# Three causal attentions of a two-block transformer: pairs of heads in a pipeline, their half-array products alternating, in a pinned order of the matrix engine

## The chip, the core and the metric

The kernel runs on one core of a Trainium2 chip. A core has a matrix engine (TensorE, called PE in the profile), a vector engine (DVE), a scalar engine (ACT), GpSimd (POOL) and a sync engine (SP) that issues most DMAs. Each engine works through its own queue in order and waits at semaphores for the others. The metric is the time of one execution on the device in microseconds (us), lower is better; the median of the runs shown counts.

## What is computed

Two transformer blocks over 256 tokens of 1024 features, in float32. Block 1: attention (16 heads of 64 features, rotary positions; with one block of keys it is plain causal attention) beside a gated recurrence, cross attention to a memory, a feed-forward net. Block 2: two layers of feed-forward, mixer, feed-forward; the first mixer is NSA, the second differential attention. The three attentions that the change touches, shortened:

```
# block 1, per head h:        p = softmax(causal(q k^T / 8));  o = p v
# NSA, 16 query heads, 4 key heads; with 256 tokens all selected and window keys are in reach:
def nsa_mixer(h, ...):
    o_cmp, o_sel = nsa_compressed_selected(q, kc, vc, ks, vs, slopes)   # 15 compressed keys; 256 keys
    o_win = banded_attention(q, kw, vw, slopes, NSA_WINDOW)             # 256 keys
    g = sigmoid(gates)
    o = g[..., 0:1] * o_cmp + g[..., 1:2] * o_sel + g[..., 2:3] * o_win
    return o @ w_out
# differential attention, 8 heads, two score maps each, values of 128:
    p = masked_softmax(sc, dist >= 0)
    a = p[:, :, 0] - lmbda * p[:, :, 1]
    o = rmsnorm(a @ v, subln) * (1 - lam_init);  return o @ w_out
```

## The kernel before

Weights of some 280 MB stream through the core once. `proj` (line 320) loads a weight tile of 512 rows by 512 columns, and for each pair of 128-row chunks ACT makes a rounded copy (`wh`, line 354), DVE the remainder (`wl`, line 355), and PE twelve products of 128x128 by 512 columns: two chunks, two token tiles, three products each (lines 330, 334, 335). `proj` is a generator that yields after each weight tile (24 products).

The attentions work per head. `softmax_causal` (line 476) makes the causal scores in two blocks, 128 queries by 128 keys and 128 by 256, into one PSUM bank ("sc", two banks in turn), with 64 features as contraction: a half of the array's rows. DVE adds the bias and finds each row's extreme in one operation (line 485), ACT takes the exponential with its row sum (line 487). Then reciprocal and scaling on DVE, three 128x128 transposes on PE (line 508) with a copy to SBUF, and P@V, whose 64 output features use a half of the array's columns. Three stages do so:

- A, `attn_a` (line 634): 16 heads, woven with the remaining chunks of `qkv` and the first inputs of the recurrence (`weave`, rate 0.6 tiles a head).
- N, `attn_n` (line 1141), called for two halves m = 0, 1 of the heads: per key head and branch two heads (`par`), 16 pairs in all; `compressed_branch` (line 1099) is a small softmax over 16 blocks for 8 heads at once, its P@V (line 1170) joins the others in bank "on".
- D, `attn_d` (line 1243), two halves of four heads: two score maps a head, combined on DVE (lines 1252 to 1254), P@V with 128 features (lines 1257 to 1259).

The order of the engines' queues is made by the framework's scheduler, which moves instructions by its own cost model, except those wrapped in `late`, which keep the program's order among themselves. Before, only a few are pinned: deferred transposes (`tick`, line 254) and two products (`hold`). So weight products, scores, transposes and P@V of neighbouring heads are mixed as the scheduler sees fit. In A, N and D the weight products that do not depend on the attention are the filler.

Of the kernel before, what the change touches and what calls it, by code (L numbers as in the profile page):

```python
# [2 lines left out]

# [14 lines left out]
P = 128  # L18
# [10 lines left out]
def shape_constants():  # L29
# [28 lines left out]
    # heads as (group pair, kv head, parity of the group): head = 4 * kv head + 2 * group pair + parity  # L58
# [25 lines left out]
def tile_kernel(ctx: ExitStack, tc: tile.TileContext, A, out):  # L84
    nc = tc.nc
    V, SC, G, T = nc.vector, nc.scalar, nc.gpsimd, nc.tensor
    late = tc.keep_in_program_order

# [22 lines left out]
    class Feat:  # L111
        """[feature, token]: chunks of 128 features by 256 tokens, four chunks to a tile, made when first used."""
# [15 lines left out]
    class Tok:  # L128
        """[token, feature]: 2 x 128 tokens by 1024 features, 512 features to a tile, made when first used."""
# [16 lines left out]

    def wk(shape, s, bufs, dt=F32):
        tag, bufs = ("w2k", NW2K) if s in W2K else (s, bufs)
        return work.tile(shape, dt, name=nm(s), tag=tag, bufs=bufs)
# [8 lines left out]
    BS = {"sc", "sx", "cs", "ch", "dc"}  # L158
# [30 lines left out]
    def load_gains():  # L189
# [10 lines left out]
        # gains of 64, twice along the row  # L200
# [17 lines left out]
    def rsqrt(ms, n):  # L218
        """1/sqrt of ms [128, n] (any positive float32), by Newton steps."""
# [27 lines left out]
    # transposes wait for the vector engines: they are queued behind matrix products that do not  # L247
# [6 lines left out]
    def tick():  # L254
        for p in pending:
            p[0] -= 1
        if pending and pending[0][0] <= 0:
            pending.pop(0)[1](late)
# [61 lines left out]
    def proj(xT, w, nchunks, evac, lead=False, rows=None, pre=None, final=False):  # L320
        """evac(n, tt, psum) for each chunk of columns of x @ w."""
# [5 lines left out]
        def products(o, c, tt, h, l):  # L327
# [3 lines left out]
            if hold[0]:  # L331
                late(first)
                hold[0] -= 1
# [6 lines left out]
        for grp in groups:  # L340
# [4 lines left out]
            for k0, nk in units:  # L345
                for n in grp:
# [4 lines left out]
                    for c0, m in [(0, 1), (1, 1), (2, 2)] if early else [(c, min(2, nk - c)) for c in range(0, nk, 2)]:  # L351
# [5 lines left out]
                        if not by_tile:  # L357
# [4 lines left out]
                            tick()  # L362
                    if k0 + nk == kc:
# [5 lines left out]

    def run(*gens):  # L370
        for g in gens:
            for _ in g:
                pass

    def weave(main, fill, rate=None, at=()):
        """Emit `rate` units of fill for each step of main (or one after each of the steps `at`), then what is left."""
        acc = 0.0
        for i, _ in enumerate(main):
            acc += at.count(i + 1) if rate is None else rate
            while acc >= 1.0:  # L380
                next(fill, None)
                acc -= 1.0
        run(fill)

# [3 lines left out]
    def residual(xT, w, alpha, g, s, lead=True, rows=None):  # L388
        """x += alpha * (xT @ w): a generator; its result holds the next normed operand (split x^T * g) and 1/rms."""
# [55 lines left out]
    def to_T(src, blocks, dst, scale=None, age=2):  # L445
        """dst(b), dst(b + 1): transposes of the blocks of src(b, tt), times scale, for pairs of blocks."""
# [11 lines left out]
    def segment_norm(ps2, rs, nseg, extra=None):  # L458
        """For psum tiles of both token tiles: 1/rms over runs of 64 of (ps * rs), times rs (and extra)."""
# [16 lines left out]
    def softmax_causal(qT, kT, bias, mscale):  # L476
        """exp(mscale * (q k + bias) - its max) per row [128, 384] and the row sums [128, 2]."""
        ps = bank("sc")
        T.matmul(ps[:, 0:128], qT[:, 0:128], kT[:, 0:128], start=True, stop=True)  # L479
        T.matmul(ps[:, 128:384], qT[:, 128:256], kT[:, 0:256], start=True, stop=True)  # L480
# [3 lines left out]
        for tt, (a, b) in enumerate(((0, 128), (128, 384))):  # L484
# [4 lines left out]
        return p, sm  # L489

# [13 lines left out]
    def transpose_p(p, evac=evac_copy):  # L504
        """[t, (t0 s0 | t1 s0 | t1 s1)] to [s, same blocks]."""
# [3 lines left out]
        pT = wk([P, 384], "pT", 3)  # L509
# [19 lines left out]
    next(qkv)  # L529
    transposed_half(xa, 1, xT1h, xT1l, g1)  # L530
    next(qkv)
# [6 lines left out]
    # rotary tables, times 1/rms: [128, tt, 32]  # L538
# [65 lines left out]
    for _ in range(4):  # L604
        next(qkv)
# [10 lines left out]
    for _ in range(2):  # L616
        next(qkv)
    transpose_gains()

    # products of gains that meet in one contraction  # L620
# [11 lines left out]
    oTah, oTal = new_xT("oa")  # L632

    def attn_a():
        for pair in range(8):
            if pair == 4:
                flush()
            o = bank("o")
            for h2 in range(2):
                r = slice(h2 * 64, h2 * 64 + 64)  # L640
                h = 2 * pair + h2
                p, sm = softmax_causal(qTa(pair)[r], kTa(pair)[r], causal, 0.125)
                ri = tn([P, 2], "ri", 6)
                V.reciprocal(ri, sm)
                V.tensor_scalar(p[:, 0:128], p[:, 0:128], ri[:, 0:1], None, op0=ALU.mult)
                V.tensor_scalar(p[:, 128:384], p[:, 128:384], ri[:, 1:2], None, op0=ALU.mult)
                pT = transpose_p(p)
                T.matmul(o[r, 0:256], va(0, h * 64, 64), pT[:, 0:256], start=True, stop=False)  # L648
                T.matmul(o[r, 128:256], va(1, h * 64, 64), pT[:, 256:384], start=False, stop=True)
                yield  # L650
            split_evac(o[:, 0:256], oTah(pair), oTal(pair))

# [10 lines left out]
    def silu_tanh(ps, tt, dst):  # L663
        """2 * silu(ps * rstd)."""
# [15 lines left out]
    class Hgrn:  # L680
        """heads 4n..4n+3."""
# [57 lines left out]
        def head(self, hh_):  # L739
            """chunks of 128 tokens by binary levels, and the pair of chunks."""  # L740
# [72 lines left out]
    weave(attn_a(), fill_a(), 0.6)  # L813
# [33 lines left out]
    def fill1():  # L847
        yield from proj(xT1, w_in, cols(8192, 9216), evac_gate(gb))
        for _ in range(4):
            next(kv)  # L850
# [15 lines left out]
    next(kv)  # L866
    next(kv)

# [13 lines left out]
    next(qx)  # L882
    next(qx)
# [82 lines left out]
    def seg_T(ps2, nseg, dup, r2, dst, scale=None):  # L966
        """Normed runs of 64 (each twice if dup), then transposed to dst."""
# [58 lines left out]
    # compressed tokens  # L1026
# [7 lines left out]
    def compress(w1):  # L1034
        """keys on rows 0..63 of the hidden layer, values on rows 64..127: (head, 16 blocks)."""
# [55 lines left out]
        # for each kv head the keys of both parities, on the diagonal  # L1091
# [7 lines left out]
    def compressed_branch(m):  # L1099
        """P of the compressed branch for 8 heads, times gate / sum, transposed: [(kv head, 32), parity, 256 t]."""  # L1100
        psc = bank("cs")
        for tt in range(2):
            for hk in range(4):
# [3 lines left out]
        # the queries carry 1/slope: times the slope of each head again  # L1107
# [8 lines left out]
        # a row that sees no block has only -1e30: all its weights become 0  # L1116
# [10 lines left out]
                        mx.rearrange("p (a r) -> p a r", r=2)[:, :, :, None].to_broadcast([P, 8, 2, 16]), ALU.mult)  # L1127
        tp = bank("pct")
# [6 lines left out]
        return pcT  # L1135
# [5 lines left out]
    def attn_n(m):  # L1141
        pcT = None
        for hk in range(4):
            o = bank("on")
            for br in range(2):
                vv = vsw[br]
                pTs = []
                for par in range(2):
                    i = 4 * hk + 2 * m + par
# [177 lines left out]
```

## Time and profile before

| | |
|---|---|
| runs, us | 1727.02, 1727.28, 1731.16; median 1727.28 |
| profiled execution, span | 1724.7 us |
| PE busy | 1702.2 us, 99% |
| DVE busy | 1078.7 us, 63% |
| ACT busy | 898.4 us, 52% |
| stage A (first scores to last P@V) | 61.8 to 146.5 us |
| stage N | 929.4 to 1027.9 us |
| stage D, from the norm of its first keys | 1449 to 1525 us |

The span is the time from the first to the last instruction of the profiled execution; the timed runs hold some 2.6 us more around it. A PE instruction of float32 is shown as two passes, so a product appears twice in a row's count; a row of the timeline with x2 or x4 stands for several instructions, and its second number is the time from the start of the first to the modelled end of the last. Neighbouring products overlap by their modelled ends, so costs are read from start to start.

### The profile page before, as it was taken

The page shows a single profiled execution, that of the slowest core. Times are in us where ns is not written, and L with a number is a line of the kernel's source. Part 1 is how long each engine was busy: PE and PEld are TensorE (multiplying, and loading weights), DVE is VectorE, ACT ScalarE, POOL GpSimd, SP SyncE. Part 2 cuts the span into 40 slices and gives each one's busy share as a digit, 9 for nine tenths or more (in the row PEclk, how much of TensorE's full clock was granted, in tenths as well). Part 3 has the DMA queues.
Part 4 walks back from the last instruction along what each step waited for, and adds up shares of the span by engine and source line. Part 5 has one row for each costly group of instructions (what it writes and reads, how often), then busy time and mean ns, then how long its engine had stood idle before and what let it go on. Part 6 is the DMA issues. An engine that isn't in the chain of part 4 may idle for free.

```text
span 1724.7 us, 21866 instructions
## 1 busy us (share of the span) xinstructions
PE 1702.2 (99%) x8170; PEld 1366.3 (79%) x8170; DVE 1078.7 (63%) x2129; ACT 898.4 (52%) x1473; POOL 29.5 (2%) x49
## 2 busy tenths in 40 slices
PE   8999999999999999999999999999999999999999
PEld 6767888878878888888877667888888887778887
DVE  6866585766465555655577766555655557975554
ACT  5566456545454445544455655444444455765442
POOL 3100000000000000000000000000000000000000
PEclk9999999999999999999999999999999999999999
DMA  8333344245445555655574115555555554345554
GB/s 296 132 122 137 126 154 171 98 147 171 158 152 177 191 172 194 195 177 190 195 238 134 50 34 172 189 187 191 183 181 185 180 191 166 123 147 189 178 183 134
DMA packets 211226, 284.12 MB, mean 165 GB/s; under 512 B 8304, under 2 KB 136032, under 8 KB 211120
## 3 DMA queue, kind: packets, MB, share of 16 engines
q1 hardware_dynamic: 209024, 278.10, 48.8%
q0 software_dynamic: 1936, 4.57, 0.8%
q8 instruction: 64, 1.05, 0.2%
q14 instruction: 42, 0.34, 0.1%
q10 hardware_dynamic: 160, 0.07, 0.0%
HBM read 281.65 MB, written 1.05 MB: 164 GB/s over the span
## 4 chain that ended last, share of the span: by engine, by line
PE 93%; DVE 3%; ACT 2%; issue 1%; DMA 0%; POOL 0%; SPq 0%; ACTq 0%; DVEq 0%; POOLq 0%
PE mm L330 26%; PE mm L335 26%; PE mm L334 26%; PE am L774 1%; PE pT L508 1%; PE ht L436 1%; PE sc L480 1%; PE xt L272 1%; PE on L1163 1%; DVE wl L355 1%; PE sc L479 1%; PE tT L452 1%; ACT wh L354 1%; PE o L648 1%; PE dc L752 0%
## 5 line engine op out<-in xcount | busy, mean ns | idle before, releaser
L355 DVE TENSOR_TENSOR wl<-raw,wh 128x1024 fp32r<-128x1024 f32 (+1 forms) x523 | 636.8, 1219 | 478.4 <-ACT wh L354 477.7
L354 ACT ACTIVATE wh<-raw 128x1024 fp32r<-128x1024 f32 (+1 forms) x523 | 549.1, 1051 | 560.1 <-PE mm L335 544.2
L330 PE MATMUL mm<-wh,hh 128*128 128x512 f32 x440 | 172.6, 392 | 0.0
L335 PE MATMUL mm<-wh,hl 128*128 128x512 f32 x440 | 171.4, 389 | 0.0
L334 PE MATMUL mm<-wl,hh 128*128 128x512 f32 x440 | 171.3, 389 | 0.0
L330 PE MATMUL mm<-wh,x1h 128*128 128x512 f32 x288 | 115.7, 405 | 0.0
L334 PE MATMUL mm<-wl,x1h 128*128 128x512 f32 x288 | 114.6, 399 | 0.9 <-DVE wl L355 0.9
L335 PE MATMUL mm<-wh,x1l 128*128 128x512 f32 x288 | 113.4, 395 | 0.0
L335 PEld LDWEIGHTS mm<-wh,hl 128*128 128x128 f32 x440 | 82.6, 188 | 17.4
L330 PEld LDWEIGHTS mm<-wh,hh 128*128 128x128 f32 x440 | 82.6, 188 | 16.9
L334 PEld LDWEIGHTS mm<-wl,hh 128*128 128x128 f32 x440 | 82.7, 188 | 16.8
L427 ACT ACTIVATE silu<-mm,rstd 128x256 f32<-128x256 f32 x110 | 51.8, 475 | 62.3 <-PE mm L335 60.2
L330 PE MATMUL mm<-wh,xeh 128*128 128x512 f32 x176 | 70.0, 398 | 1.1 <-ACT xeh L280 1.1
L330 PE MATMUL mm<-wh,xbh 128*128 128x512 f32 x176 | 70.0, 398 | 1.1 <-ACT xbh L280 1.1
L330 PE MATMUL mm<-wh,xfh 128*128 128x512 f32 x176 | 69.7, 398 | 1.1 <-ACT xfh L280 1.1
L330 PE MATMUL mm<-wh,xch 128*128 128x512 f32 x176 | 69.8, 397 | 0.0
L330 PE MATMUL mm<-wh,xnh 128*128 128x512 f32 x176 | 69.6, 395 | 0.0
L335 PE MATMUL mm<-wh,xnl 128*128 128x512 f32 x176 | 68.7, 390 | 0.0
L334 PE MATMUL mm<-wl,xnh 128*128 128x512 f32 x176 | 68.7, 390 | 0.0
L334 PE MATMUL mm<-wl,xeh 128*128 128x512 f32 x176 | 68.7, 390 | 0.0
L335 PE MATMUL mm<-wh,xcl 128*128 128x512 f32 x176 | 68.6, 390 | 0.0
L334 PE MATMUL mm<-wl,xch 128*128 128x512 f32 x176 | 68.6, 390 | 0.0
(429 smaller groups left out, 3335.3 us busy)
## 6 DMA issues: line engine op xcount, KB each, us to landing
raw<-in_ffn_w_in_dram SPq DMA_DIRECT2D x176, 512.0 KB, 4.6
raw<-in_ffn_w_out_dram SPq DMA_DIRECT2D x40, 1024.0 KB, 4.8
raw<-in_w_in_dram SPq DMA_DIRECT2D x35, 1024.0 KB, 4.8
raw<-in_w_ffn_in_dram SPq DMA_DIRECT2D x44, 512.0 KB, 4.5
raw<-in_diff_w_in_dram SPq DMA_DIRECT2D x12, 1024.0 KB, 5.0
raw<-in_w_ffn_out_dram SPq DMA_DIRECT2D x10, 1024.0 KB, 4.8
raw<-in_wkv_x_dram SPq DMA_DIRECT2D x8, 1024.0 KB, 5.0
raw<-in_w_br_attn_dram SPq DMA_DIRECT2D x4, 1024.0 KB, 4.8
```

What stands on the lines that cost most here:

```text
L272: pin(T.transpose(tp[:, cc * 256 + tt * P:cc * 256 + (tt + 1) * P], src(tt, (c0 + cc) * P, P), ident))
L330: first = T.matmul(o, a, h, start=(c == 0), stop=False)
L334: T.matmul(o, a, l, start=False, stop=False)
L335: T.matmul(o, b, h, start=False, stop=(c == kc - 1))
L354: SC.activation(wh[:, :m, :wd], raw[:, c0:c0 + m, :wd], AF.Copy)
L355: V.tensor_tensor(wl[:, :m, :wd], raw[:, c0:c0 + m, :wd], f32(wh[:, :m, :wd]), ALU.subtract)
L427: SC.activation(s_, ps[:, 0:256], AF.Silu, scale=rs[:, tt:tt + 1])
L436: pin(T.transpose(tp[:, cc * 256 + t2 * P:cc * 256 + (t2 + 1) * P], hs[n, t2][:, cc * P:(cc + 1) * P], ident))
L452: pin(T.transpose(tp[:, i * 256 + tt * P:i * 256 + (tt + 1) * P], src(b + i, tt), ident))
L479: T.matmul(ps[:, 0:128], qT[:, 0:128], kT[:, 0:128], start=True, stop=True)
L480: T.matmul(ps[:, 128:384], qT[:, 128:256], kT[:, 0:256], start=True, stop=True)
L508: T.transpose(tp[:, b * P:(b + 1) * P], p[:, b * P:(b + 1) * P], ident)
```

## The change

`T` becomes a wrapper of the matrix engine with a flag `strict`; while it is set, every matrix product and transpose is pinned in program order. `weave_parts` sets it and gives, after each step of the attention, a number of parts of the filler from a table; `proj` now yields a part after each pair of chunks (12 products) too. `scores_pair` makes the scores of two heads into two banks, the heads' halves alternating. `pipeline` runs over pairs: transposes of pair i, scores and softmax of pair i+1, P@V of pair i-1, then the filler. P@V alternates the two heads' column halves. `transpose_p` has six SBUF buffers instead of three; some work tiles move to another pool, and bank "cs" to the other pair of banks. Comments and docstrings are dropped.

```
+    class Tensor:
+        strict = False
+        def matmul(self, *a, **k):
+            ins = nc.tensor.matmul(*a, **k)
+            return late(ins) if self.strict else ins
...
+    def weave_parts(main, fill, after):
+        T.strict = True
+        for i, _ in enumerate(main):
+            for _ in range(after[i] if i < len(after) else 0):
+                next(fill, None)
+        run(fill)
+        T.strict = False
...
+    def scores_pair(q, k):
+        banks = [bank("sc") for _ in range(2)]
+        for tt, (a, b) in enumerate(BLOCKS):
+            for h2 in (1, 0):
+                r = slice(h2 * 64, h2 * 64 + 64)
+                T.matmul(banks[h2][:, a:b], q[r, tt * P:(tt + 1) * P], k[r, 0:(tt + 1) * P], start=True, stop=True)
+        return banks
...
+    def pipeline(n, soft, trans, apply):
+        ps = {0: soft(0)}
+        yield
+        pTs = {}
+        for i in range(n + 1):
+            if i < n:
+                pTs[i] = trans(i, ps.pop(i))
+            if i + 1 < n:
+                ps[i + 1] = soft(i + 1)
+            if i:
+                apply(i - 1, pTs.pop(i - 1))
+            yield
...
-        pT = wk([P, 384], "pT", 3)
+        pT = wk([P, 384], "pT", 6)
...
+        def apply(pair, pTs):
+            o = bank("o")
+            for st, (a, b) in enumerate(((0, 256), (256, 384))):
+                for h2 in range(2):
+                    h = 2 * pair + h2
+                    T.matmul(o[h2 * 64:h2 * 64 + 64, a // 2:256], va(st, h * 64, 64), pTs[h2][:, a:b],
+                             start=(st == 0), stop=(st == 1))
...
-    weave(attn_a(), fill_a(), 0.6)
+    weave_parts(attn_a(), fill_a(), [3, 2, 3, 2, 3, 2, 3, 2, 1, 0])
...
-    weave(attn_n(0), nsa_in, at=(4, 16))
+    weave_parts(attn_n(0), nsa_in, [1, 0, 1, 0, 1, 0, 1, 0, 0, 0])
...
-    weave(attn_n(1), part(out_g, 2), at=(8, 16))
+    weave_parts(attn_n(1), islice(out_g, 4), [1, 0, 0, 1, 0, 0, 1, 0, 0, 1])
...
-    weave(attn_d(0), diff_in, 1.25)
+    weave_parts(attn_d(0), diff_in, [3, 2, 2, 2, 1, 0])
...
-    weave(attn_d(1), last_part(out_g), 0.25)
+    weave_parts(attn_d(1), islice(out_g, 4), [1, 0, 0, 1, 0, 0])
```

What it does to PE's queue is shown at three places. The names: `mm` weight products, `sc` scores, `pT` transposes of P, `on` and `od` P@V, `tT` transposes of queries or keys; numbers tell buffers apart. In the changed kernel every product has the wrapper's line, L95, and every transpose L99.

In stage N, third pair of heads on, PE's queue before:

```order
L508 MATMUL pT_7932<-ident,p_7920 128x128 x3
L1163 MATMUL on_7849<-pT_7915,vsw_7846 64x256
L479 MATMUL sc_8063<-kTs_7693,qTn_7493 128x128
L480 MATMUL sc_8063<-kTs_7693,qTn_7493 128x256
L479 MATMUL sc_8084<-kTs_7693,qTn_7493 128x128
L1163 MATMUL on_7849<-pT_7936,vsw_7846 64x256
L1163 MATMUL on_7849<-pT_7915,vsw_7846 64x128
L1163 MATMUL on_7849<-pT_7936,vsw_7846 64x128
L480 MATMUL sc_8084<-kTs_7693,qTn_7493 128x256
```

and after:

```order
L99 MATMUL pT_8031<-ident,p_7984 128x128 x3
L99 MATMUL pT_8037<-ident,p_7996 128x128 x3
L95 MATMUL sc_8044<-kTs_7693,qTn_7493 128x128
L95 MATMUL sc_8043<-kTs_7693,qTn_7493 128x128
L95 MATMUL sc_8044<-kTs_7693,qTn_7493 128x256
L95 MATMUL sc_8043<-kTs_7693,qTn_7493 128x256
L95 MATMUL on_8073<-pT_7906,vsw_7517 64x256
L95 MATMUL on_8073<-pT_7912,vsw_7517 64x256
L95 MATMUL on_8073<-pT_7906,vsw_7517 64x128
L95 MATMUL on_8073<-pT_7912,vsw_7517 64x128
L95 MATMUL on_8073<-pT_7970,vsw_7846 64x256
L95 MATMUL on_8073<-pT_7976,vsw_7846 64x256
```

Transposes, scores and P@V, which were mixed head by head and with weight products, now stand in blocks of one kind, two heads alternating.

At the start of stage D, between the transposes of its first keys and its first scores, PE's queue before (of the weight products ahead of these rows, over thirty stand behind the key chunk's last one):

```order
L334 MATMUL mm_12204<-wl_12302,xdh_11867 128x512
L335 MATMUL mm_12204<-wh_12301,xdl_11869 128x512
L452 MATMUL tT_12145<-ident,tok_12141 128x128
L452 MATMUL tT_12152<-ident,tok_12141 128x128
L330 MATMUL mm_12203<-wh_12301,xdh_11867 128x512
L334 MATMUL mm_12203<-wl_12302,xdh_11867 128x512
L452 MATMUL tT_12145<-ident,tok_12143 128x128
L452 MATMUL tT_12145<-ident,tok_12141 128x128
```

and after, from the middle of the eight transposes, which now directly follow the key chunk's last product:

```order
L99 MATMUL tT_12145<-ident,tok_12143 128x128
L99 MATMUL tT_12152<-ident,tok_12143 128x128
L99 MATMUL tT_12152<-ident,tok_12141 128x128
L99 MATMUL tT_12152<-ident,tok_12143 128x128
L95 MATMUL sc_12159<-kTd_12150,qTd_12060 128x128
L95 MATMUL sc_12158<-kTd_12150,qTd_12060 128x128
L95 MATMUL sc_12159<-kTd_12150,qTd_12060 128x256
L95 MATMUL sc_12158<-kTd_12150,qTd_12060 128x256
L95 MATMUL mm_12187<-wh_12191,xdh_11637 128x512
L95 MATMUL mm_12187<-wl_12192,xdh_11637 128x512
```

The weight products of the next chunk, which stood ahead of the transposes, have moved behind the scores.

In the second half of stage D, from the second head's scores on, PE's queue before:

```order
L479 MATMUL sc_12726<-kTd_12653,qTd_12534 128x128
L480 MATMUL sc_12726<-kTd_12653,qTd_12534 128x256
L479 MATMUL sc_12736<-kTd_12653,qTd_12534 128x128
L480 MATMUL sc_12736<-kTd_12653,qTd_12534 128x256
L334 MATMUL mm_12890<-wl_12897,odh_12429 128x512
L335 MATMUL mm_12890<-wh_12896,odl_12431 128x512
L330 MATMUL mm_12891<-wh_12896,odh_12429 128x512
L334 MATMUL mm_12891<-wl_12897,odh_12429 128x512
L335 MATMUL mm_12891<-wh_12896,odl_12431 128x512
L330 MATMUL mm_12890<-wh_12896,odh_12429 128x512
L479 MATMUL sc_12786<-kTd_12653,qTd_12534 128x128
```

and after:

```order
L99 MATMUL pT_12732<-ident,p_12687 128x128 x3
L95 MATMUL sc_12739<-kTd_12644,qTd_12423 128x128
L95 MATMUL sc_12738<-kTd_12644,qTd_12423 128x128
L95 MATMUL sc_12739<-kTd_12644,qTd_12423 128x256
L95 MATMUL sc_12738<-kTd_12644,qTd_12423 128x256
L99 MATMUL pT_12767<-ident,p_12744 128x128 x3
L95 MATMUL sc_12774<-kTd_12644,qTd_12423 128x128
L95 MATMUL sc_12773<-kTd_12644,qTd_12423 128x128
L95 MATMUL sc_12774<-kTd_12644,qTd_12423 128x256
L95 MATMUL sc_12773<-kTd_12644,qTd_12423 128x256
L95 MATMUL od_12802<-vd_12668,pT_12736 128x128 x3
L99 MATMUL pT_12812<-ident,p_12779 128x128 x3
```

Between one head's scores and its transposes there now stand only another head's P@V, or nothing, and no weight products.

## Rows read from the trace of the kernel before

**Rows 1.** Page, part 1: busy us, share, instructions.
```profile
PE 1702.2 (99%) x8170; PEld 1366.3 (79%) x8170; DVE 1078.7 (63%) x2129; ACT 898.4 (52%) x1473; POOL 29.5 (2%) x49
```

**Rows 2.** Stretches A, N, D: length, engines' busy us, clock, DMA share, GB/s.
```profile
61.80:146.50 84.70, 83.15 (x410) 57.55 (x409) 56.87 (x164) 50.69 (x113) 5.13 (x4) 1.00 0.30 102
929.40:1027.90 98.50, 97.88 (x552) 62.14 (x552) 68.80 (x332) 63.38 (x192) 0.00 (x0) 1.00 0.16 54
1449.00:1525.00 76.00, 74.92 (x393) 57.07 (x391) 68.68 (x259) 51.74 (x143) 0.00 (x0) 1.00 0.37 125
```

**Rows 3.** Timeline of PE in A: start, duration, engine, line, operation, count.
```profile
74.91 0.40 PE L330 MATMUL mm<-wh,x1h 128*128 128x512 f32 x1
75.24 0.65 PE L648 MATMUL o<-pT,va 128*64 128x256 f32 x2
75.72 0.38 PE L649 MATMUL o<-pT,va 128*64 128x128 f32 x2
...
76.37 0.39 PE L335 MATMUL mm<-wh,x1l 128*128 128x512 f32 x1
```

**Rows 4.** Timeline of PE in D: two heads' scores, together and then in turn.
```profile
1498.05 0.50 PE L479 MATMUL sc<-kTd,qTd 64*128 64x128 f32 x4
...
1498.91 0.50 PE L330 MATMUL mm<-wh,odh 128*128 128x512 f32 x1
1499.70 0.48 PE L479 MATMUL sc<-kTd,qTd 64*128 64x128 f32 x2 [0.29 <-DVE nb L485]
...
1501.11 0.50 PE L334 MATMUL mm<-wl,odh 128*128 128x512 f32 x1
```

**Rows 5.** Timeline of all engines in N: the steps of the softmax chain.
```profile
1012.94 0.34 DVE L1156 TENSOR_SCALAR p<-p,ri 128x256 f32<-128x256 f32 x1
...
1013.40 0.55 PE L508 MATMUL pT<-ident,p 128*128 128x128 f32 x3
...
1013.88 0.65 PE L1163 MATMUL on<-pT,vsw 128*64 128x256 f32 x2
...
1014.43 0.39 ACT L487 ACTIVATE p<-p,nb 128x128 f32<-128x128 f32 x1
...
1014.82 0.50 ACT L487 ACTIVATE p<-p,nb 128x256 f32<-128x256 f32 x1
...
1015.22 0.19 ACT L487 ACTIVATION_READ_ACCUMULATOR p<-p,nb 128x1 f32 x1
...
1015.75 0.16 DVE L1153 RECIPROCAL ri<-sum 128x2 f32<-128x2 f32 x1
...
1016.34 0.35 DVE L1156 TENSOR_SCALAR p<-p,ri 128x256 f32<-128x256 f32 x1
...
1016.36 0.50 PE L479 MATMUL sc<-kTs,qTn 64*128 64x128 f32 x4
...
1017.31 0.29 DVE L485 CUSTOM_DVE_ANT_0 p<-sc,ndist 128x128 f32<-128x128 f32 x1 [0.62 <-PE sc L480]
...
1017.64 0.40 ACT L487 ACTIVATE p<-p,nb 128x128 f32<-128x128 f32 x1
```

**Rows 6.** Timeline of all engines ahead of D's first scores: the key norm.
```profile
1449.60 1.37 ACT L464 ACTIVATE sq<-mm,rstd 128x512 f32<-128x512 f32 x2 [0.98 <-PE mm L335]
...
1452.04 1.23 DVE L355 TENSOR_TENSOR wl<-raw,wh 128x1024 fp32r<-128x1024 f32 x1
...
1457.39 0.41 PE L452 MATMUL tT<-ident,tok 128*128 128x128 f32 x2 [0.35 <-DVE tok L977]
...
1459.37 0.50 PE L479 MATMUL sc<-kTd,qTd 64*128 64x128 f32 x4
```

**Rows 7.** Timeline of POOL ahead of A's first scores: the last rotary keys.
```profile
57.82 2.54 POOL L580 TENSOR_TENSOR tok<-ta,tb 128x512 f32<-128x512 f32 x2 [9.14 <-DVE tb L578]
```

**Rows 8.** Timeline of PE at the start of the run: weight products.
```profile
9.80 1.05 PE L334 MATMUL mm<-wl,x1h 128*128 128x512 f32 x2
...
11.71 0.62 PE L334 MATMUL mm<-wl,x1h 128*128 128x512 f32 x2
```

More of the change, by code (lines that the diff above doesn't have):

```diff
@@ L2 @@
 from contextlib import ExitStack
+from itertools import islice
 import numpy as np
@@ L350, in proj @@
                     parts = []
[L351 removed]
+                    sizes = [(0, 1), (1, 1), (2, 2)] if early else [(c, min(2, nk - c)) for c in range(0, nk, 2)]
+                    for i, (c0, m) in enumerate(sizes):
                         wh = splitp.tile([P, 2, 512], F32R, name=nm("wh"), tag="wh", bufs=NSPLIT)
@@ L368, in proj, with unit @@
                     yield
+    def unit(g):
+        while next(g, None) == "part":
+            pass
     def run(*gens):
@@ L616, in tile_kernel @@
     for _ in range(2):
-        next(qkv)
+        unit(qkv)
     transpose_gains()
@@ L634, in attn_a, with soft @@
     def attn_a():
-        for pair in range(8):
+        def soft(pair):
             if pair == 4:
                 flush()
[L638 to L642, printed above, removed]
+            ps = []
+            for bk in scores_pair(qTa(pair), kTa(pair)):
+                p, sm = softmax_causal(bk, causal, 0.125)
                 ri = tn([P, 2], "ri", 6)
                 V.reciprocal(ri, sm)
[L645 to L650, printed above, removed]
+                scale_rows(p, ri)
+                ps.append(p)
+            return ps
+        def apply(pair, pTs):
[5 more added lines that the diff above has]
+                             start=(st == 0), stop=(st == 1))
             split_evac(o[:, 0:256], oTah(pair), oTal(pair))
+        yield from pipeline(8, soft, lambda _, ps: [transpose_p(p) for p in ps], apply)
     rsh = cpool.tile([P, 2], F32, name="rsh")
@@ L849, in fill1 @@
         for _ in range(4):
-            next(kv)
+            unit(kv)
             yield
@@ L1141, in attn_n, with soft @@
     def attn_n(m):
-        pcT = None
-        for hk in range(4):
+        held, pc, cb = {}, [], compressed_branch(m)
+        def soft(j):
+            hk, br = divmod(j, 2)
+            ps = []
+            for par, bk in enumerate(scores_pair(qTn(4 * m + hk), kTs[br][:, hk, :])):
+                p, sm = softmax_causal(bk, ndist, 2.0 ** (-8.0 * (4 * hk + 2 * m + par + 1) / 16))
+                ri = tn([P, 2], "ri", 6)
+                V.reciprocal(ri, sm)
+                V.tensor_tensor(ri, ri, gates[:, :, hk, m, par, 1 + br], ALU.mult)
+                scale_rows(p, ri)
+                ps.append(p)
+            if j == 1:
+                next(cb)
+            return ps
@@ L1194, in tile_kernel @@
                             rows=lambda k0, nk: w_o.rearrange("(h g p) n -> g p h n", g=2, p=P)[k0 // 4])
-    def part(g, n):
-        for _ in range(n):
-            next(g)
-            yield
-    weave(attn_n(1), part(out_g, 2), at=(8, 16))
+    weave_parts(attn_n(1), islice(out_g, 4), [1, 0, 0, 1, 0, 0, 1, 0, 0, 1])
     xh, xl, rs = finish((out_g, out_r))
```

111 lines of the change are left out of this document (53 added, 58 removed).

## Prediction, made before the changed kernel ran

> **What bounds the kernel now.** I read the page's first part, then the busy times of three stretches, then single rows of the timeline. The page [rows 1] is to be read as: TensorE (PE) is busy for 1702.2 of 1724.7 us, so a change can gain only by making PE's own work shorter, and loses whenever it makes PE wait. The change touches three attentions. [Rows 2] are their stretches: A (block 1's causal attention), N (the NSA mixer), D (the differential attention). In all three PE has little idle time (1.5, 0.6 and 1.1 us) at granted clock 1.00, while VectorE (DVE) and ScalarE (ACT) are 60 to 90% busy. So the present order hides long chains on DVE and ACT behind PE work.
>
> How PE loses time inside its busy time is in [rows 3, 4]. In A a weight product follows the next after 0.23 us. From the product at 74.91 to the one at 76.37 there are two such intervals (0.46) and one head's P@V; that leaves 1.00 us. The P@V is four passes: the two wide ones take 0.48 us to the first narrow one (75.24 to 75.72), so I reckon 0.22 for a wide and half for a narrow one, 0.65 in all. The other 0.35 us is the way from a whole-array product to a half-array one and back: **about 0.17 us a switch**. [Rows 4] show what two heads in the two halves save: both heads' scores together take 0.86 us (1498.05 to 1498.91), one after the other 1.41 (1499.70 to 1501.11): **0.55 us a pair**. For P@V of two heads, halves alternating, the same reckoning gives one head's 0.65 us a pair.
>
> **The change part by part, as work.** It does the same arithmetic, in another order of PE. In the order I counted the switches between whole, row-half and column-half products: 54 become 26 in A, 104 become 42 in N, 22 become 16 in D.
> A: 28 x 0.17 = 4.8, and 8 pairs of P@V x 0.65 = 5.2, since before they run one head at a time [rows 3]; scores mostly ran together already. 10 us less work.
> N: 62 x 0.17 = 10.5, 16 pairs of P@V x 0.65 = 10.4, 16 pairs of scores x 0.55 = 8.8; 29.7, at most, because some scores already run as four together (1016.36 in [rows 5]). I take 29.
> D: 6 x 0.17, and a little from the scores: 1.7.
> So the work falls by some 41 us. If it were only that, the kernel would be 1687 us.
>
> **What is added: waits.** Within the three stages every PE instruction is pinned in the written order, and the written order has one pair of heads in flight: transposes of pair i, scores of i+1, P@V of i-1, then a portion of weight products ("part", 12 x 0.23 = 2.7 us). The next transposes wait for the whole softmax of a pair. [Rows 5] give that chain in N, from rows of different heads: scores' start to first reduction 0.95 (1016.36, 1017.31); to the first exponential 0.33; four exponentials on ACT, whose queue takes them one by one: 0.39 for the narrow one with its sum (1014.43 to 1014.82), about 0.50 for the wide one, together 1.8, and 0.2 for the last sum; from the reciprocal to the last scaling 0.59 (1015.75 to 1016.34) and from that scaling to its transposes 0.46 (1012.94 to 1013.40). 0.95 + 0.33 + 1.8 + 0.2 + 0.59 + 0.46 = 4.3 us, and 0.48 us for three transposes and a switch: the next scores start **4.8 us** after the last ones. PE's own work in such a cycle is 0.86 + 0.33 + 0.48 = 1.7 us, 1.9 more with P@V and 2.9 more with a part and its switch.
>
> *Stage A.* A step has 2 or 3 parts (5.5 to 8.2 us), more than the chain. That is enough cover; within the steps I charge nothing (0 to 2 us in the range). But the first scores are now pinned ahead of the stage's weight products: 12 of them stood between before and covered GpSimd's work on the last rotary keys, which ends at 60.36 [rows 7]. Uncovered, 12 x 0.23 = 2.8 us. With before's own 1.5 us of idle gone: -10 - 1.5 + 2.8 = **-8.7 us** (-12 to -4).
>
> *Stage N.* 16 cycles have 8 parts between them, one of which stands after the last cycle. 7 cycles with a part are nearly full (0.3 us idle each, 2.1); 5 with P@V alone idle 4.8 - 1.7 - 1.9 = 1.2 (6.0); 4 bare ones 3.1 (12.4). The compressed branch's dozen small DVE operations enter the queue in one cycle of each half, 1.4 each (2.8). The query norm of the second half of heads lands in the bare end of the first half: two squares, two reductions, a dozen small operations, two scalings, as in [rows 6] from 1449.60 to 1457.39 less two weight splits, 5.3 us, of which I charge 5. The start, where compressed keys and their transposes no longer stand behind products, 3, and the ends of both halves 1. Sum 32.3. Against 29 saved and 0.6 us of old idle: **+2.7 us** (-10 to +9; the sum is a difference of two large numbers).
> [...]
>
> *Stage D.* Start: between the key chunk's last product and the first scores, before runs over thirty weight products (counted in its order; the first scores are at 1459.37 in [rows 6]), while DVE does the key norm. Now they are pinned behind the scores. The norm needs 7.8 us (1449.60 to 1457.39); the DVE order leaves one weight split of 1.2 us (1452.04) in it instead of two, so 6.6, then the copy to SBUF between transposes and scores: PE waits about 7 us. In the first half the parts (3, 2, 2, 2, 1) cover the chain. In the second half there are 2 parts in 4 cycles; the chain there has two fused multiply-adds more and comes to about 5.0, from transposes to transposes about 5.5. Idle: 1.2 (a part in it) + 4.1 (scores only) + 3.2 (scores and one od) + 0.6 (a part) = 9.1, less 0.6 because the last products overlap. So 7 + 8.5 - 1.7 - 1.1 (old idle) = **+12.7 us** (+5 to +17).
>
> Nothing changes in DMA (the same issues in the same order), in the number of activation table loads, or outside the three stages. The larger pT and "hid" pools only free buffers earlier: 0.
>
> Sum: -8.7 + 2.7 + 12.7 = +6.7. I round down to **+6**, since the cover by work of the other queue is always a little better than a chain added up from rows of different heads. The profiled execution spans 1724.7 us, 2.6 below the median of 1727.28; 1724.7 + 6 + 2.6 = 1733.
>
> **Rivals.** (1) *The chains are shorter than I add up*: the first head's transposes go while the second's softmax runs, DVE and ACT overlap two heads, the query norm is done before it is needed. 9 uncovered cycles in N at 4.2 instead of 4.8 give 5.4, the norm 5, D's second half 2: 1733 - 12 = 1721. For it: in before each engine runs two heads interleaved [rows 5]; against it: ACT's four exponentials alone are 1.8 us and nothing else can start the next pair. [...]
> [...]
> (3) *The change doesn't do what it says*: excluded by the order, which has the alternation in every pair.
>
> **How the numbers follow.** Forecast (1726 to 1739): 0.45. Rival 1 (1711 to 1726): 0.29. Rival 2 (1739 to 1748): 0.21. Elsewhere 0.05. The range 1713 to 1746 leaves out the outer parts of both rivals and those 0.05. A measurement here tells about 0.3% (5.2 us) from no change: faster than 1722.1 is most of rival 1, 0.24; slower than 1732.5 is more than half of the forecast and rival 2, 0.47; the rest, 0.29, is the same.
>
> **What would show it.** Right: PE idle of about 7 us before D's first scores and 3 us before A's; in N scores of successive bare pairs 4.8 us apart and PE some 70% busy; A shorter by 8 to 9 us. [...]

## The result, and the profile after

The changed kernel takes 1755.71 us (median of 4 runs, 1753.37 to 1756.18) against 1727.38 for the kernel before in the same comparison: ratio 1.0158, 95% interval 1.0145 to 1.0170, **slower by 28 us**. The direction is the forecast one; the size is not, and the time lies 10 us above the range.

Page of the kernel after, parts 1, 2 and 4, answering [rows 1]: busy us and shares, then the busy tenths of PE and the granted clock in 40 slices of 43.8 us, then the chain that ended last.

```profile
PE 1689.1 (96%) x8170; PEld 1368.9 (78%) x8170; DVE 1086.5 (62%) x2129; ACT 896.6 (51%) x1473; POOL 30.3 (2%) x49
...
PE   8999999999999999999997799999999998799999
...
PEclk9999999999999999999998899999999999899999
...
PE 88%; DVE 6%; ACT 4%; issue 1%; DMA 0%; POOL 0%; SPq 0%; ACTq 0%; DVEq 0%; POOLq 0%
```

PE is busy for 13 us less than in [rows 1], and yet the kernel is longer: idle time rose by more than the work fell. It sits in slices 22, 23, 34 and 35, which are N and D. There the clock row, 9 everywhere before, shows an 8 as well.

To compare kernels I cut the run at events that all of them share: A from the transposes of the gains to the recurrence's first product, N from the compressed tokens' transposes to the first product of the next feed-forward net, D from its first weight product to the next feed-forward net's. Columns: stretch; length; busy us (and instructions) of PE, PEld, DVE, ACT, POOL; granted clock; DMA share; GB/s. Before:

```profile
57.46:165.77 108.31, 106.67 (x520) 76.30 (x519) 69.83 (x184) 63.92 (x132) 7.67 (x6) 1.00 0.35 122
929.41:1040.01 110.60, 108.87 (x600) 70.81 (x601) 75.68 (x341) 69.64 (x203) 0.54 (x1) 1.00 0.19 61
1415.06:1533.57 118.51, 116.21 (x582) 90.56 (x580) 98.76 (x323) 77.28 (x181) 0.00 (x0) 1.00 0.42 143
```

After:

```profile
57.75:163.36 105.61, 98.44 (x520) 75.95 (x519) 69.93 (x184) 62.88 (x132) 8.43 (x6) 0.97 0.38 125
927.04:1046.78 119.74, 98.86 (x600) 69.04 (x600) 79.41 (x341) 69.13 (x203) 0.54 (x1) 0.89 0.18 56
1421.81:1562.08 140.27, 119.94 (x582) 93.68 (x580) 102.33 (x323) 77.02 (x181) 0.00 (x0) 0.91 0.37 121
```

A is 2.7 us shorter, N 9.1 longer, D 21.8 longer: together 28.2 of the 28.7 us by which the span grew. Nothing outside the stages moved: between them every event keeps its distance. The clock is below 1.00 in all three.

Stretches at granted clock 0.50 in the kernel after, the same columns (six of the eight stretches, 51 of 58 us):

```profile
60.37:67.20 6.83, 6.46 (x22) 4.73 (x23) 4.40 (x21) 3.06 (x10) 0.27 (x1) 0.50 0.07 28
...
930.77:937.60 6.83, 3.98 (x18) 2.77 (x18) 2.69 (x15) 2.84 (x5) 0.00 (x0) 0.50 0.30 115
947.84:951.25 3.41, 3.15 (x14) 2.18 (x13) 3.13 (x17) 2.08 (x9) 0.00 (x0) 0.50 0.00 0
...
995.62:1005.86 10.24, 7.52 (x34) 4.58 (x34) 6.70 (x32) 4.13 (x14) 0.00 (x0) 0.50 0.25 84
...
1459.83:1466.66 6.83, 3.40 (x16) 2.37 (x16) 3.40 (x15) 1.33 (x2) 0.00 (x0) 0.50 0.19 75
1521.27:1538.34 17.07, 10.10 (x43) 6.69 (x41) 8.51 (x41) 5.89 (x28) 0.00 (x0) 0.50 0.13 45
```

Outside the eight stretches the granted clock is 1.00. Weight products stand 0.43 us apart in the first of them (65.31 to 65.74) and 0.23 just behind it, at 1.00 (67.56 to 67.79). All eight together hold 41.4 us of PE busy time; by these two intervals that work would take about half at 1.00. So, as an estimate, the clock can explain 20.7 us at the very most, if no wait would take its place.

What PE waited for, as the trace sums it (engine, line and tile waited for; us in total, times, longest), in the stretches N and D of the kernel after:

```profile
PE pT L99 <- DVE p L535: 11.6, 13, 1.7
PE kct L99 <- DVE ax L1148: 3.4, 1, 3.4
PE pT L99 <- DVE rs_t L243: 1.9, 1, 1.9
PE co L95 <- DVE cht L1134: 1.2, 1, 1.2
```

```profile
PE pT L99 <- DVE p L1321: 10.7, 3, 3.7
PE tT L99 <- DVE tok L1042: 6.9, 3, 6.1
```

These are the waits of the prediction by name: transposes for the softmax's last scaling (L535, L1321), compressed keys (`kct`), the query norm (`rs_t`), D's key norm (`tok`, 6.1 us in one piece). In the kernel before PE is idle for 1.7 us in this N.

### The profile page after: what moved, and what is told of

It reads as the page before. It is cut to its first block, busy times and chain, and to the rows that moved or that the text cites. A ratio compares the mean times of both kernels' runs of the same rounds, so it can differ in the third digit from the quotient of the medians.

```text
span 1753.4 us, 21902 instructions
## 1 busy us (share of the span) xinstructions
PE 1689.1 (96%) x8170; PEld 1368.9 (78%) x8170; DVE 1086.5 (62%) x2129; ACT 896.6 (51%) x1473; POOL 30.3 (2%) x49
## 3 DMA queue, kind: packets, MB, share of 16 engines
q8 instruction: 64, 1.05, 0.2%
HBM read 281.65 MB, written 1.05 MB: 161 GB/s over the span
## 4 chain that ended last, share of the span: by engine, by line
PE 88%; DVE 6%; ACT 4%; issue 1%; DMA 0%; POOL 0%; SPq 0%; ACTq 0%; DVEq 0%; POOLq 0%
PE mm L95 77%; DVE wl L373 2%; PE am L95 2%; PE sc L95 1%; PE ht L99 1%; ACT wh L372 1%; PE xt L99 1%; PE tT L99 1%; PE pT L99 1%; PE dc L95 1%; ACT p L529 1%; PE on L95 1%; DVE p L535 1%; DVE p L527 0%; PE ch L95 0%
## 5 line engine op out<-in xcount | busy, mean ns | idle before, releaser
L95 PE MATMUL mm<-wh,hh 128*128 128x512 f32 x440 | 172.8, 393 | 0.0
L95 PE MATMUL mm<-wh,hl 128*128 128x512 f32 x440 | 171.6, 390 | 0.0
L95 PE MATMUL mm<-wl,hh 128*128 128x512 f32 x440 | 171.5, 390 | 0.0
L95 PE MATMUL mm<-wh,x1h 128*128 128x512 f32 x288 | 116.5, 408 | 0.0
L95 PE MATMUL mm<-wl,x1h 128*128 128x512 f32 x288 | 114.6, 399 | 0.9 <-DVE wl L373 0.9
L95 PE MATMUL mm<-wh,x1l 128*128 128x512 f32 x288 | 113.7, 396 | 0.0
L95 PEld LDWEIGHTS mm<-wh,hl 128*128 128x128 f32 x440 | 82.7, 188 | 17.4
L95 PEld LDWEIGHTS mm<-wl,hh 128*128 128x128 f32 x440 | 82.7, 188 | 16.8
L95 PEld LDWEIGHTS mm<-wh,hh 128*128 128x128 f32 x440 | 82.7, 188 | 16.7
L529 ACT ACTIVATE p<-p,nb 128x128 f32<-128x128 f32 (+1 forms) x128 | 56.7, 444 | 37.5 <-DVE nb L527 37.5
L95 PE MATMUL mm<-wh,xbh 128*128 128x512 f32 x176 | 70.1, 399 | 1.1 <-ACT xbh L297 1.1
L95 PE MATMUL mm<-wh,xeh 128*128 128x512 f32 x176 | 70.1, 399 | 1.1 <-ACT xeh L297 1.1
L95 PE MATMUL mm<-wh,xfh 128*128 128x512 f32 x176 | 69.8, 399 | 1.1 <-ACT xfh L297 1.1
L95 PE MATMUL mm<-wh,xch 128*128 128x512 f32 x176 | 69.9, 397 | 0.0
L95 PE MATMUL mm<-wh,xnh 128*128 128x512 f32 x176 | 69.7, 396 | 0.0
L95 PE MATMUL mm<-wh,xnl 128*128 128x512 f32 x176 | 68.8, 391 | 0.0
L95 PE MATMUL mm<-wl,xnh 128*128 128x512 f32 x176 | 68.8, 391 | 0.0
L95 PE MATMUL mm<-wh,xcl 128*128 128x512 f32 x176 | 68.7, 391 | 0.0
L95 PE MATMUL mm<-wl,xch 128*128 128x512 f32 x176 | 68.7, 390 | 0.0
```

Of the source, the lines that this page charges most:

```text
L95: ins = nc.tensor.matmul(*a, **k)
L529: SC.activation(p[:, a:b], p[:, a:b], AF.Exp, scale=-1.0, bias=nb[:, tt:tt + 1], accum_out=sm[:, tt:tt + 1])
```

## Experiments

In every run the events between the stages keep their distances to 0.2 us, so one run tells about all three. All lengths are of the stretches above, as difference to the kernel before (A, N, D), in us; the time is that of the run or the median. `warm`, `lead`, `early`, `earlead` and `unpin` ran once, `b2`, `b3` and `noalt` twice; `b1` ran twice beside these three (1705.4 us) and four times later (1703.1, in the table). The kernel before took 1727.0 to 1728.9 us in these comparisons.

| kernel | A | N | D | time |
|---|---|---|---|---|
| after | -2.7 | +9.1 | +21.8 | 1755.7 |
| warm: idle products in the waits | -5.4 | +6.0 | +20.0 | 1746.4 |
| lead: weight products in three waits | -7.4 | +9.6 | +16.7 | 1745.4 |
| early: next scores ahead of the transposes | -0.6 | +5.4 | +15.7 | 1747.7 |
| earlead: both | -2.3 | +4.1 | +14.3 | 1743.2 |
| unpin: no pinning | -10.3 | -13.5 | +6.5 | 1709.7 |
| b1: no pinning, D as before | -10.4 | -13.5 | +0.1 | 1703.1 |
| b2: b1, score maps alternating in D | -10.4 | -13.5 | +1.9 | 1704.5 |
| b3: b1, next scores ahead | -10.9 | -12.9 | +0.1 | 1705.0 |
| noalt: b1 without alternation in A, N | -10.2 | -10.3 | +0.1 | 1706.5 |

The theories: W, the waits themselves are the loss; C, the waits bring the clock down and that is the loss; and, once both had been looked at, whether pinning, pairing or alternation makes the difference.

**warm**

```
+    def spin(reg, n):
+        for _ in range(n):
+            late(T.matmul(reg, ident, ident, start=True, stop=True))
...
         tp = bank("pT")
+        spin(tp[:, 384:512], warm)
```

> The changed kernel, plus idle work for the array: 128x128 products of the identity, which nobody reads, pinned ahead of the products that waited longest in N (at its start and in the bare cycles, some 14 us in all) and in D (26 passes pairs, 5.7 us, ahead of its first keys' transposes, 3 us ahead of each head's transposes in its second half). Stage against before, in the changed kernel: A -2.4, N +9.1, D +21.7 us. Theory W (the waits themselves are the loss, the lower clock is incidental): N and D stay within 2 us of these. Theory C (the waits bring the array to the lower of its two levels, and what follows takes twice as long): the granted clock stays 1.00 in N and D, and N falls to about +2 (-2 to +5), D to about +14 (11 to 17); total about 1741 us.

The clock stayed up: 1.00 in A and D, 0.99 in N. N fell by 3.1 and D by 1.8 only. In D one batch of idle products overhung: the last scaling starts at 1528.33 and takes 0.74, but PE was in its batch until the transposes at 1531.25.

```profile
1523.75 0.93 PE L95 MATMUL sc<-kTd,qTd 64*128 64x128 f32 x8
1524.61 0.94 PE L95 MATMUL od<-vd,pT 128*128 128x128 f32 x6
1528.12 3.29 PE L95 MATMUL pT<-ident 128*128 128x128 f32 x28
1531.25 0.49 PE L99 MATMUL pT<-ident,p 128*128 128x128 f32 x3
```

About 2.2 us of D are therefore the experiment's own. In A nothing had been added and PE was idle for as long (7.5 us, 7.2 in the kernel after), but this time the granted clock was 1.00 and not 0.97, and A was 2.7 us shorter. So the clock cost some 2.7 in A, 3.2 in N, 4 in D, **about 10 of the 28 us** (an estimate from these differences). The rest, 18 us, stays at full clock: W has the larger part, C the smaller one, and neither number expected for N and D (C: +2 and +14) was reached.

**lead**

```
+    next(qkv)
     flush()
...
     steps(diff_in, 6)
+    for _ in range(3):
+        next(diff_in)
     flush()
-    weave_parts(attn_d(0), diff_in, [3, 2, 2, 2, 1, 0])
+    weave_parts(attn_d(0), diff_in, [2, 2, 2, 1, 0, 0])
...
-    weave_parts(attn_d(1), islice(out_g, 4), [1, 0, 0, 1, 0, 0])
+    weave_parts(attn_d(1), islice(out_g, 4), [1, 1, 0, 1, 0, 0])
```

> The changed kernel with weight products moved into three of its waits: one part ahead of A's first scores (and one less after), three parts ahead of D's first scores (the table behind them 2, 2, 2, 1), and one part more in the second half of D (1, 1, 0, 1 for 1, 0, 0, 1). N is unchanged, +9.1. Theory W: A gains its uncovered 2.5 us, D the 6.1 us of wait at its start and 2 to 3 of the second half: A -5, D +13, total about 1744. Theory C: also the stretches at the lower clock behind these waits go (60.4 to 67.2 in A, 1459.8 to 1466.7 in D), 3 us each: A -8, D +9, total about 1737.

A came to -7.4 with no low clock (1.00), C's number; D to +16.7, between the kernel after and W's +13. D's first half gained 4.2 of the 6.1 us that W expected there (its last weight product, counted from D's start). Its second half gained 0.9, although it had a part more: so there it was not work that was missing.

**early**

```
-            if i < n:
-                pTs[i] = trans(i, ps.pop(i))
             if i + 1 < n:
                 ps[i + 1] = soft(i + 1)
+            if i < n:
+                pTs[i] = trans(i, ps.pop(i))
```

> The changed kernel with the next pair's scores ahead of this pair's transposes in the pinned order, in all three stages, so that two softmax chains can be under way. If latency of one pair in flight is the bound (my forecast's mechanism), the bare cycles of N shrink from some 6 us to ACT's work on a pair, 2.8 to 3.5: N from +9.1 to about -8 (-14 to -2), and D's second half loses 4 to 8 us less: total about 1733. Rival: the queues of ACT and DVE (weight splits and copies put between the softmax's steps) are the bound: N and D stay within 4 us of the changed kernel.

D's second half gained almost 7 us, as expected, N 3.7 where 17 were expected. So one pair in flight is a cause, but two in flight do not free the stage; N stays within the 4 us of the rival, the queues of ACT and DVE, but no run shows that cause by itself. A lost 2 us instead: PE was idle for 8.7 us there, against 7.2. **earlead** puts both together:

> Pinned as the changed kernel, with both repairs: weight products in three waits (as lead) and the next scores ahead of the transposes (as early). If the repairs add up by stage: A -8, N +5, D +2 in its first half and +8 in its second: total about +7 against before, 1736 us; pinning then costs some 30 us against the same code unpinned (b3). Rival: repaired waits keep the clock up everywhere and overlap more: total at or below before's 1728.

The repairs do not add up: +16 in sum instead of +7. The pinned order stays far above the kernel before; the rival is out.

**unpin**

```
     def weave_parts(main, fill, after):
-        T.strict = True
+        T.strict = False
```

> The changed kernel with pinning off: the same code order, pairs, parts and alternation, but the scheduler may move PE's instructions in all three stages. If the pinning is the cause, waits go: A -5 to -10, N 0 to -15, D 0 to +3, total 1705 to 1728. Rival: the code order itself (one pair in flight, transposes ahead of the next scores) is the cause, and the scheduler keeps it or fills it no better: N and D stay over +5 each.

**This one line is worth 46 us** (1755.7 against 1709.7, a single run). Same pairs, same parts, same alternation in the code, but the scheduler may move PE's instructions: A -10.3, N -13.5. The windows of the kernel show PE full again, at full clock in A and N:

```profile
57.68:155.69 98.01, 97.50 (x519) 74.16 (x519) 69.24 (x184) 62.59 (x132) 8.64 (x6) 1.00 0.41 134
919.38:1016.53 97.15, 93.59 (x601) 65.22 (x601) 74.81 (x341) 67.96 (x203) 0.54 (x1) 1.00 0.22 68
1391.55:1516.56 125.01, 119.30 (x581) 92.60 (x580) 100.01 (x323) 77.69 (x181) 0.00 (x0) 0.97 0.42 137
```

PE idle is 0.5 us in A and 3.6 in N, against 7.2 and 20.9 in the kernel after. D is still 6.5 us longer than before: its parts are used up before its last heads are normed, and PE waits 2.3 us for that norm, with 6.8 us of low clock behind it (0.97 in D).

**b1** (no pinning, D head by head with its old weave)

> Pinning off, and the differential attention written as before the change (head by head, its old weave); A and N keep pairs, parts and alternation. If the stages are independent, it sums the stages of the runs so far: A -10.1, N -13.4, D 0 to -1 against before: about 1704 us (1701 to 1707). If D's loss without pinning (+6.5) came from something outside its code (buffers of P, moved tiles), D stays at +3 or more: 1708 or above.

1705.4 us in its first runs, and 1703.07 in four more, ratio 0.9860 to the kernel before, interval 0.9843 to 0.9876: **24 us faster than before, 52 faster than the change as made.** The stages add: D is back at +0.1, so nothing outside D's own code had lengthened it. What of the gain comes from the pairs, and what from the finer parts of the filler, the six buffers of P or the moved tiles, no run separates.

> The same kernel as b1, timed in more rounds for its interval: ratio to the kernel before 0.987 (0.985 to 0.989).

**b2** alternates the two score maps of D's heads:

```
-            p0, s0 = one(slice(0, 64))
-            p1, s1 = one(slice(64, 128))
+            (p0, s0), (p1, s1) = [softmax_causal(bk, ndist, 2.0 ** -(h + 1)) for bk in scores_pair(qTd(h), kTd(h))]
```

> As b1, but the two score maps of a differential head alternate in the two row halves. If scores in turn cost 0.55 us a pair wherever they stand, D gains up to 4 us over b1 (8 heads; some ran together already): D -2 to -4. Rival: PE's order there is mixed by the scheduler anyway and DVE is the busier engine in D (68.7 of 76 us): within 1 us of b1.

No gain: D is 1.8 us longer where 2 to 4 less were expected. The time (1704.5) is not longer than `b1`'s beside it (1705.4), but the profile of that `b1` had lost 2.6 us more ahead of stage A, where the two kernels are the same. **b3** writes the next scores ahead of the transposes, as `early`, unpinned:

> As b1, with the next pair's scores written ahead of this pair's transposes (A and N). If the scheduler follows the code's order and chains of one pair still bound N, N gains 2 to 6 us over b1 (-13.4 to -16 or below). Rival: unpinned, the scheduler already issues scores as banks come free, and the code order tells little: within 2 us of b1 in A and N.

A gains 0.6, N loses 0.6: the code's order tells little once the scheduler may choose.

**noalt** takes the alternation out of A and N:

```
-        for tt, (a, b) in enumerate(BLOCKS):
-            for h2 in (1, 0):
+        for h2 in (0, 1):
+            for tt, (a, b) in enumerate(BLOCKS):
...
-            for st, (a, b) in enumerate(((0, 256), (256, 384))):
-                for h2 in range(2):
+            for h2 in range(2):
+                for st, (a, b) in enumerate(((0, 256), (256, 384))):
```

> As b1, but without the alternation: each head's scores and P@V stand together, in pairs as before in the code. If the two halves running side by side is what saves (my 0.65 us a pair of P@V and 0.55 a pair of scores), A loses 4 to 6 us against b1 (-10.1 to about -5) and N 10 to 19 (-13.4 to about 0). Rival: grouping by kind alone (fewer switches) does it, or the engine lets a later head's product run beside an earlier one in the other half anyway: A and N within 2 us of b1.

A is the same to 0.1 us: writing the halves in alternation is worth nothing there. N loses 3.2 us, of which at most 1.7 may be the clock (granted clock 0.98 in N: one stretch of 3.4 us at 0.50); its trace has 74 switches between halves and whole array, b1's 60. Timeline of PE in A, of noalt and of b1's second run: scores and P@V of a pair, then weight products.

```profile
76.49 0.88 PE L95 MATMUL o<-pT,va 128*64 128x256 f32 x8
77.30 0.50 PE L95 MATMUL mm<-wh,x1h 128*128 128x512 f32 x1
77.64 0.40 PE L95 MATMUL mm<-wl,x1h 128*128 128x512 f32 x1
```

```profile
77.81 0.87 PE L95 MATMUL o<-pT,va 128*64 128x256 f32 x8
78.61 0.51 PE L95 MATMUL mm<-wh,x1h 128*128 128x512 f32 x1
78.95 0.40 PE L95 MATMUL mm<-wl,x1h 128*128 128x512 f32 x1
```

From the first pass of P@V to the second product behind it: 1.15 us for two heads written one after the other, 1.14 for two alternating, and 1.13 for a single head in [rows 3] (75.24 to 76.37). In these three places the second head, as the neighbour, costs 0.01 to 0.02 us.

`noalt` is not pinned, and its queue is not on record; that the scheduler left the heads as they are written is not shown. But the same can be read where the queue is on record, in stage N of the kernel before (first queue under "The change"): there one head's wide scores (L480) stand ahead of the next head's narrow ones (L479), two passes each. The trace starts a narrow pass of the next head (the third in the first row) at 950.41, 0.01 us ahead of the first wide pass and 0.22 ahead of the second, and the next head's second pass at 950.63, with the second wide pass:

```profile
950.09 0.70 PE L479 MATMUL sc<-kTs,qTn 64*128 64x128 f32 x3
950.42 0.38 PE L480 MATMUL sc<-kTs,qTn 64*128 64x256 f32 x1
950.63 0.27 PE L479 MATMUL sc<-kTs,qTn 64*128 64x128 f32 x1
950.63 0.38 PE L480 MATMUL sc<-kTs,qTn 64*128 64x256 f32 x1
```

So products for the two halves ran side by side here without standing in alternation.

## Why the prediction was wrong, point by point

The forecast's mechanism was right: the pinned order has one pair in flight, PE waits for softmax chains, and A's gain is eaten by N and D. Its sum was +6; at full clock the stages give -5.4, +6.0 and about +18, so +18, and the low clock adds about 10. Two steps failed above all: the sum held nothing for the clock (10 of the 22 us that it missed), and D's second half was put at 8.5 us of waits where some 12 were found. A missed 3 us by inner waits that were put at nothing, and N 3 us by work saved that was put too high, most of it made up for by waits put too high as well.

- **Work saved.** A: 10 us forecast; PE's busy time fell from 106.7 to 95.5 us in `warm`, where A's clock was full, so 11. D: 1.7 forecast; in `warm` 132.4 us less 163 idle passes of 0.11 is 114.5, against 116.2: 1.7. **N: 29 forecast, 16.5 found by busy time** (106.9 us less 132 idle passes is 92.4, against 108.9). The mis-sized term is the P@V: I charged 0.65 us for each of 16 pairs as if heads ran one at a time, which I had read in A's rows. In N the code before already wrote both heads' P@V together, in alternation (lines 1160 to 1164), and the halves already ran side by side. The second row below, three products of two heads, takes 0.79 us to the next product (951.73), as long as one head's two products in stage A (75.24 to 76.03); only the first wide product of each pair stood alone (0.58). Little was left to save but the switches.

```profile
949.51 0.65 PE L1163 MATMUL on<-pT,vsw 128*64 128x256 f32 x2
...
950.94 0.86 PE L1163 MATMUL on<-pT,vsw 128*64 128x256 f32 x6
```

  The 0.55 us a pair of scores was misread as well. In [rows 4] the second scores were late not because they stood behind the first: their first product waits for DVE to have read their PSUM bank, which ends at 1500.20, and starts at 1500.26:

```profile
1500.12 0.08 DVE L485 DVE_READ_ACCUMULATOR2_ANT nb<- 128x1 f32 x1
```

```profile
1500.26 0.48 PE L479 MATMUL sc<-kTd,qTd 64*128 64x128 f32 x2
```

  So that price is one of free banks, not of alternation. Counted from each group's start to the next product, switches included, N's scores fell from 23.6 us before to 14.8 in `warm` and its P@V from 25.7 to 15.5, so 19 us by this count, also far from 29.
- **N's waits.** 32 us of idle forecast, 24 found in `warm`. The chain was well sized: scores of successive pairs start 4.6 to 5.6 us apart at full clock (4.8 forecast, 6.2 with the compressed branch; 6.2 and 6.3 found), apart from one cycle of 6.4 and the joint of the two halves with the query norm, 11.3. Idle is smaller by what the work is larger, because the chain sets the length of a cycle, not the work. Hence N at +6.0 against +2.7, a miss of 3 us, with two terms each wrong by 8 to 12.
- **A's waits.** Forecast 2.8 us of uncovered products at the start and nothing inside the steps. Inside there were four waits of 0.9 to 1.0 us, and none of them is for a softmax. Transposes of queries, keys and P go through the same two PSUM banks in turn (`bank`); the next transposes wait until ACT has copied a bank out, and in all four cases ACT had a weight split of 1.06 us ahead of that copy. PE's order may no longer go around the wait. In `warm` A was idle for 7.5 us in all, where the sum has 2.8.

```profile
92.52 1.06 ACT L372 ACTIVATE wh<-raw 128x1024 fp32r<-128x1024 f32 x1 [1.66 <-issue]
93.49 0.58 ACT L487 ACTIVATE qTa<-tT 128x512 f32<-128x512 f32 x1
```

```profile
94.12 0.55 PE L99 MATMUL pT<-ident,p 128*128 128x128 f32 x3 [0.92 <-ACT qTa L487]
```

- **D's start.** 7 us forecast, 6.1 found in one piece, answering [rows 6]:

```profile
1463.12 2.05 PE L99 MATMUL tT<-ident,tok 128*128 128x128 f32 x8 [6.13 <-DVE tok L1042]
1465.31 1.56 PE L95 MATMUL sc<-kTd,qTd 64*128 64x128 f32 x8
```

  The scores behind it took 1.50 us to the next product, against 0.86 in [rows 4], at granted clock 0.50; for the weight products behind them it was 1.00 (1466.7 to 1469.0).
- **D's second half: a step that failed.** I took 5.5 us from transposes to transposes, four times. Found, at full clock in `warm`, between successive scores: 8.3, 5.3 and 5.7; in the kernel after 8.3, 5.9 and 7.4:

```profile
1520.19 0.74 PE L99 MATMUL pT<-ident,p 128*128 128x128 f32 x3 [3.74 <-DVE p L1321]
...
1525.86 0.99 PE L99 MATMUL pT<-ident,p 128*128 128x128 f32 x3 [3.69 <-DVE p L1321]
...
1533.30 0.99 PE L99 MATMUL pT<-ident,p 128*128 128x128 f32 x3 [3.28 <-DVE p L1321]
```

  In the first chain, weight splits of later parts stand on ACT and DVE between its own steps; the first line of each fence is the split, the second the softmax's step behind it:

```profile
1516.55 1.06 ACT L372 ACTIVATE wh<-raw 128x1024 fp32r<-128x1024 f32 x1
1517.51 0.49 ACT L529 ACTIVATE p<-p,nb 128x256 f32<-128x256 f32 x1
```

```profile
1517.64 1.23 DVE L373 TENSOR_TENSOR wl<-raw,wh 128x1024 fp32r<-128x1024 f32 x1 [1.17 <-ACT wh L372]
1518.78 0.16 DVE L1317 RECIPROCAL ri<-sum 128x2 f32<-128x2 f32 x1
```

  In the third, ACT waits for the previous head's P@V, with three of the pair's exponentials behind it in its queue:

```profile
1530.12 0.28 ACT L1332 ACTIVATE ax<-od 128x128 f32<-128x128 f32 x1 [0.80 <-PE od L95]
...
1530.38 0.50 ACT L529 ACTIVATE p<-p,nb 128x256 f32<-128x256 f32 x1
```

  I had built the chain from durations and left out what the scheduler, which still orders ACT and DVE, puts between its links. Against 8.5 us forecast the second half, from the first half's last weight product to D's end, lost 15.3 us in the kernel after and 14.5 in `warm`, so some 12 at full clock without the 2.2 us of the overhang.
- **The clock: the step that failed by most.** A falling clock was rival 2 (1739 to 1748, at 0.21). What it would cost was my estimate, and no run shows that term: in the kernel before the granted clock is 1.00 in all three stretches, and also where two weight products take 1.05 us instead of 0.62 [rows 8]. What the runs showed in its place: eight stretches at 0.50 in the kernel after, 58.0 us long, at a cost of about 10 us (the estimate from `warm`), and some of them behind short waits, as at 947.84 after waits of 1.7 and 0.5 us, with three transposes between. The rival and the forecast were treated as alternatives, so the sum holds nothing for the clock; they add, and the range, made from each by itself, ended 10 us too low. In `warm` the granted clock was 1.00 in A and D and 0.99 in N (3.4 us at 0.50), and N and D still lost; so the clock is the largest part of the forecast's miss, but not of the kernel's loss.

  The granted clock was 0.50 behind waits of the kernel after, and 1.00 in D of `warm`, where idle products filled the waits (0.91 in D of the kernel after). That the fall is not certain shows in A: in the kernel after it came at 60.37, within the second of two waits of 1.4 and 0.8 us; in `warm`, with the same products in A and 7.5 us idle there against 7.2, it did not come (1.00 against 0.97).
- **What I did not weigh.** That the pinning, not the new order of the code, is the part that costs (`unpin`). The prediction priced work saved and waits added as if both came with the change; the unpinned kernel has nearly all of the first and little of the second. What is not settled is how D could gain: no version of it that ran was shorter than before.

## What to carry to other kernels

Put work of one kind (whole array, row half, column half), and work for both halves of the array, next to each other in the queue: here PE's busy time fell by 11 us in A and 16.5 in N (`warm` against before), and two neighbouring heads' P@V took 1.14 us where one head's took 1.13. Where the second head's scores waited for a PSUM bank, in [rows 4], the two heads' took 1.41 us instead of 0.86. The order inside made 0.1 us in A and at most 3.2 us in N. Do not pin the busiest engine's whole order around a chain through other engines when only parts of that order matter: a pinned queue turned delays on the other engines into idle time of the bound one (20.9 us in N, against 3.6 unpinned). To price such a chain, count what else stands in those engines' queues between its links, and add the clock to the waits (about 10 us here, an estimate), not beside them.

## What the runs showed of the hardware that was not expected

- Two heads' half-array products written one head after the other took 0.81 us (76.49 to 77.30 in noalt), as long as alternating ones (0.80, 77.81 to 78.61 in b1).
- That an engine works through its queue in order, as the document says at its start, shows in two waits of the kernel after: PE was idle for 6.1 us ahead of the key transposes at 1463.12, with weight products behind them in its queue, and ACT for 0.80 us ahead of 1530.12, with an exponential behind it whose input was done at 1529.14. It does not hold to the letter for the two halves of the array: in the kernel before, whose queue is on record, a narrow pass of one half started at 950.41, the two passes of the wide product of the other half that stood before it at 950.42 and 950.63.
- The granted clock fell here at waits of 0.5 to 1.7 us with small products between them (1.4 and 0.8 us at 60.37, 1.7 and 0.5 at 947.84), and one kernel's run had such a fall where another's with the same products and as much idle time had none (A: 0.97 in the kernel after, 1.00 in `warm`); A was 2.7 us longer with it.
- Of 20.7 us that the low clock could have cost, about 10 appeared (both estimates from the rows above). PE was also idle for 16.6 us within these stretches (58.0 less 41.4), so slow products may have taken the place of waits; no run shows it by itself.
